# Activation, queries and keys transposed by Vector in 32x32 blocks and through DRAM, in a two-layer encoder

## The chip, the cores and the metric

The kernel runs on one core of a Trainium2 chip. The metric is the device time of one execution in microseconds, as the median of three runs; lower is better.

## The reference

Two layers act on x of 256 tokens by 2048. Each has a token mixer of four head groups and a SwiGLU channel mixer, both between RMS norms and with a residual:

```python
for l in range(DEPTH):
    h = rmsnorm(x, norm_mix_pre[l])
    proj = h @ w_in[l]
    a_q, a_k, a_v, b_glu, c_q, c_k, c_v, d_q, d_k, d_v = jnp.split(proj, split_at, axis=-1)
    out_a = diff_attention(a_q, a_k, a_v, diff_lambda[l], diff_subln[l], l)
    out_b = conformer_conv(b_glu, conv_dw[l], conv_dw_b[l], conv_ln_g[l], conv_ln_b[l],
                           conv_pw[l], conv_pw_b[l])
    out_c = gqa_axial_attention(c_q, c_k, c_v, gqa_q_norm[l], gqa_k_norm[l])
    out_d = neighbourhood_attention(d_q, d_k, d_v, na_rpb[l])
    mixed = jnp.concatenate([out_a, out_b, out_c, out_d], axis=-1) @ w_out[l]
    x = x + rmsnorm(mixed, norm_mix_post[l])
    h = rmsnorm(x, norm_ffn_pre[l])
    f = (jax.nn.silu(h @ ffn_gate[l]) * (h @ ffn_up[l])) @ ffn_down[l]
    x = x + rmsnorm(f, norm_ffn_post[l])
```

Groups A (differential attention, two maps of 64 per head), C (4 query heads over 2 key heads, normed and with rotary positions) and D (a neighbourhood window with a learned bias) have 4 heads of 128 each; B is a gated depthwise convolution of 31 taps over 512 channels, followed by a 512x512 product (`conv_pw`). The hidden width of the channel mixer is 5632. Everything is float32.

## The kernel before

All large products are weights times activations, in single-pass fp32r. Each weight is split into a high and a low part, each activation too, and three of the four products are summed in PSUM. The weights stream from DRAM: a `Raw` load (L201) brings two blocks of 128 rows by 1024 columns (1 MB; SP's queue, L214); `split_hi` (L222) makes the high part on Scalar (the names `whi`), `split_lo` (L231) the low part on Vector (`wlo`). A **unit** is one block of 128 x 1024, a **step** (L67) one unit times one tile of 128 tokens: six products of 128 x 512 (`products`, L297).

A layer runs four phases: the input projection in five column pairs in the order B, C, A, D, V, each 16 units by 2 token tiles (160 steps, written out at L1051); the output projection (two pairs, blocks in the order C, B, A, D in the first, L1062); gate and up (11 pairs of 512 columns of each, L1069); down (two pairs over 44 blocks, L1075). `run` (L345) walks through the steps. At each it calls the functions attached to the step (`pre`), advances the generators of the side work by one stretch (`tick`, L318), issues splits up to 7 units ahead (`NSPLIT`, `splits_to`, L242), which in turn issue the loads, and then the step's products. Where a step's activation isn't made yet, the planner's own clock is moved on (`wait`, L334). No engine reorders what it is given: the order in which Python emits is the order of each engine's queue, SP's included.

The generators do the side work: `norm_c`, `rope_a`, `evac_d` and `evac_v` (L827, L726, L921, L966) take a projected pair out of PSUM into the tiles `rotC`, `rotA`, `rotD`, `vAD`; `attn_c`, `attn_a`, `attn_d` (L863, L784, L934) transpose queries and keys and start a generator per head (`head_c`, `head_a`, `head_d`), which does scores (banks `sc`), softmax, and the transposes of the probabilities (`probs_transposed`, L771). A `yield` hands over until the next tick. Two PSUM banks each serve scores (`sc`) and transposes and small products (`tp`), two generators holding them in turn (`claim`, L148).

Queries and keys are needed with the head dimension on the partitions, and come out of the projection with the tokens there. `heads_transposed` (L752) has TensorE transpose four blocks of 128x128 into a `tp` bank, which Scalar copies into the tile `qkC`, `qkA` or `qkD`:

```python
for h in range(n):
    nc.tensor.transpose(b[:, h], src(tok)[:, h * P:(h + 1) * P], self.ident)
yield
nc.scalar.activation(dst[:, 0:n, tok * P:(tok + 1) * P], b[:, 0:n], AF.Copy)
```

In the channel mixer, `ffn_half` (L531) makes h of one 512-column block and one token tile. Vector then transposes it by 16 operations of 32x128 each (`quadrants`, L548), four between two yields; `split_hi_lo` (L194) turns the result `ht` into the two parts of `hT[j]`, which the down projection reads.

The convolution's weights (`pw`) and the position bias of group D (`load_bias`, L599, 16 small transfers, attached to step 108; `mask_bias`, L614, on Vector at step 120) go through SP's queue among the weights. SBUF has 14 large **slots** of 8 KB a partition (`slot`, L135), handed out in turn; the pool of temporaries has 4 buffers of 2 KB (`tmp`, L138), and the discarded output of a sum of squares (`junk`, L417) two of its own.

Of the kernel before, what the change touches and what calls it, by code (L numbers as in the profile page):

```python
# [11 lines left out]
F32 = mybir.dt.float32  # L12
# [7 lines left out]
P = 128  # L20
L = 2
S = 256
# [80 lines left out]
class Trunk:  # L103
    def __init__(self, ctx, tc, a):
# [10 lines left out]
        self.tp = pool("temps", 4)  # L115
# [301 lines left out]
    def square_sum(self, src, out, n=(512,), bias=0.0):  # L417
        junk = self.tp.tile([P] + list(n), mybir.dt.bfloat16, tag="junk", bufs=2, name=self.name("junk"))
        self.nc.scalar.activation(junk, src, AF.Square, bias=bias, accum_out=out)
# [111 lines left out]
    def ffn_half(self, phase, j, tok):  # L531
# [14 lines left out]
        self.mark("h", phase[1], j, tok)  # L546

    def quadrants(self, dst, src, q):  # L548

        qs = slice(32 * q, 32 * q + 32)  # L550
        for r in range(4):
            rs = slice(32 * r, 32 * r + 32)
            self.nc.vector.transpose(dst[qs, :, rs], src[rs, :, qs])
# [198 lines left out]
    def heads_transposed(self, dst, src, n):  # L752

        nc = self.nc
        for tok in range(T):
            yield from self.claim("tp")
            b = self.bank("tp", (4, P))
            for h in range(n):
                nc.tensor.transpose(b[:, h], src(tok)[:, h * P:(h + 1) * P], self.ident)
            yield  # L760
            nc.scalar.activation(dst[:, 0:n, tok * P:(tok + 1) * P], b[:, 0:n], AF.Copy)
            yield
            self.free("tp")
# [20 lines left out]
    def attn_a(self):  # L784
        qk = self.slot([2, 4, S], F32, "qkA")
        for i in range(2):
            yield from self.heads_transposed(qk[:, i], lambda t: self.rotA[:, t, i], 4)
        self.ptA = self.slot([4, T, S], F32, "ptA")
        work = self.slot([2, 2, T, S], F32, "workA")
        for h in range(4):  # L790
            yield from self.until(h - 1, "done_a", self.l)
            self.spawn(self.head_a(h, qk, work[:, h % 2]))
            yield

    def head_a(self, h, qk, p):
# [3 lines left out]
        for t in range(T):  # L799
            for m in range(2):  # L800
                rows = slice(m * 64, (m + 1) * 64)
                nc.tensor.matmul(banks[m][:, t], qk[rows, 0, h, t * P:(t + 1) * P], qk[rows, 1, h],
# [60 lines left out]
    def attn_c(self):  # L863
        qk = self.slot([6, S], F32, "qkC")
# [292 lines left out]
```

## Time and profile before

| | |
|---|---|
| median of 3 runs | 2179.55 us (2179.14 to 2179.74) |
| the profiled execution | 2179.21 us, of which the span of its trace is 2177.4 us |
| instructions in the trace | 25660 |
| HBM read, written | 414.40 MB, 8.39 MB (194 GB/s over the span) |
| POOL busy | 28.7 us, 38 instructions |
| DMA queue of the transfers, share of 16 engines | 56.5% |

The span runs from the first to the last recorded instruction; the execution's own time has some 1.8 us around it. Line numbers of instructions are nearly all L89, the helper through which every engine operation is issued, so groups are told apart by the names of their tiles: `acc<-whi,xT` is a product into an accumulator, `tp<-ident,rotD` a transpose of group D's queries or keys into a bank.

### The profile page before, as it was taken

To read this page: it belongs to the slowest core of one execution; us is meant where nothing else is said; L and a number is where in the kernel's file an instruction comes from. 1 tells how busy PE (TensorE), PEld (TensorE's weight loads), DVE (VectorE), ACT (ScalarE), POOL (GpSimd) and SP (SyncE) were. 2 spreads that over 40 slices of the span, in tenths; PEclk is the share of its full clock that TensorE was granted. 3 is DMA by queue.
4 is the path that set the end of the run, shared out by engine and by line. 5 is a ranking of instruction groups with operands and counts; after the bars stand their busy time and mean duration, and the time that the engine had idled before them with its cause. 6 is when DMAs were issued, how large, how long until landed. Compare 5 with 4: busy or idle time off the path is not lost.

```text
span 2177.4 us, 25660 instructions
## 1 busy us (share of the span) xinstructions
PE 2156.2 (99%) x9720; PEld 1780.7 (82%) x9720; DVE 1459.9 (67%) x2202; ACT 1083.2 (50%) x1420; POOL 28.7 (1%) x38
## 2 busy tenths in 40 slices
PE   8999999999999999999999999999999999999998
PEld 6888887888888888888878888878888888888886
DVE  5898555777777777444468975556677777764444
ACT  5556754544444444343465576554444444443432
POOL 0000000000000000000000000000000000000000
PEclk9999999999999999999999999999999999999999
DMA  7556446655555555555575553556555655555553
GB/s 281 197 173 181 171 148 222 210 196 193 193 194 194 193 194 194 213 193 194 211 238 186 188 186 135 208 189 222 193 191 180 209 193 193 179 208 213 193 216 132
DMA packets 170013, 424.46 MB, mean 195 GB/s; under 512 B 18593, under 2 KB 19105, under 8 KB 167585
## 3 DMA queue, kind: packets, MB, share of 16 engines
q1 hardware_dynamic: 169744, 422.79, 56.5%
q8 instruction: 76, 1.25, 0.2%
q14 instruction: 49, 0.39, 0.1%
q10 hardware_dynamic: 144, 0.03, 0.0%
HBM read 414.40 MB, written 8.39 MB: 194 GB/s over the span
## 4 chain that ended last, share of the span: by engine, by line
PE 96%; ACT 2%; DVE 1%; DMA 1%; issue 1%; SPq 0%; DVEq 0%; POOLq 0%; ACTq 0%
PE acc L89 92%; PE tp L89 3%; PE sc L89 1%; DMA raw<-in_w_in_dram 1%; ACT whi L89 1%; ACT workA L89 0%; ACT L89 0%; DVE xT L89 0%; DVE mx L89 0%; DVE wlo L89 0%; DVE x L89 0%; ACT xT L89 0%; ACT conv L89 0%; ACT qkD L89 0%; ACT junk L89 0%
## 5 line engine op out<-in xcount | busy, mean ns | idle before, releaser
L89 PE MATMUL acc<-whi,xT 128*128 128x512 f32 x4096 | 1292.9, 393 | 7.4 <-DVE xT L89 2.9
L89 PEld LDWEIGHTS acc<-whi,xT 128*128 128x128 f32 x4096 | 769.3, 188 | 172.3 <-DVE xT L89 5.5
L89 PE MATMUL acc<-wlo,xT 128*128 128x512 f32 x2048 | 798.7, 390 | 0.5 <-DVE wlo L89 0.5
L89 DVE SCALAR_TENSOR_TENSOR wlo<-raw,gains,whi 128x1024 fp32r<-128x1024 f32 x512 | 641.4, 1280 | 146.9 <-ACT whi L89 141.2
L89 ACT ACTIVATE whi<-raw,gains 128x1024 fp32r<-128x1024 f32 x512 | 574.7, 1147 | 269.6 <-PE acc L89 243.1
L89 DVE TENSOR_TENSOR wlo<-raw,whi 128x1024 fp32r<-128x1024 f32 x240 | 293.3, 1224 | 256.9 <-ACT whi L89 240.1
L89 PEld LDWEIGHTS acc<-wlo,xT 128*128 128x128 f32 x2048 | 385.1, 188 | 78.4 <-DVE wlo L89 1.0
L89 PE MATMUL acc<-whi,hT 128*128 128x512 f32 x1408 | 434.1, 389 | 0.0
L89 ACT ACTIVATE whi<-raw 128x1024 fp32r<-128x1024 f32 x240 | 253.6, 1060 | 296.1 <-PE acc L89 295.2
L89 PEld LDWEIGHTS acc<-whi,hT 128*128 128x128 f32 x1408 | 264.3, 188 | 54.9
L89 PE MATMUL acc<-wlo,hT 128*128 128x512 f32 x704 | 273.9, 389 | 0.0
L89 DVE STREAM_TRANSPOSE ht<-h 32x128 f32<-32x128 f32 x704 | 213.1, 303 | 10.9
L89 PEld LDWEIGHTS acc<-wlo,hT 128*128 128x128 f32 x704 | 132.1, 188 | 27.3
L89 ACT ACTIVATE hT<-ht 128x512 fp32r<-128x512 f32 x44 | 27.8, 632 | 244.3 <-DVE ht L89 244.3
L89 DVE SCALAR_TENSOR_TENSOR h<-acc,rstd,h 128x512 f32<-128x512 f32 x44 | 32.9, 747 | 110.8 <-ACT h L89 110.7
L89 DVE SCALAR_TENSOR_TENSOR conv<-uT,lc,conv 128x256 f32<-128x256 f32 x240 | 99.2, 477 | 0.0
L89 ACT ACTIVATE h<-acc,rstd 128x512 f32<-128x512 f32 x44 | 30.3, 688 | 81.6 <-PE acc L89 81.3
L89 DVE TENSOR_TENSOR hT<-ht,hT 128x512 fp32r<-128x512 f32 x44 | 30.4, 692 | 26.6 <-ACT hT L89 26.5
L89 ACT ACTIVATE junk<-acc 128x512 bf16<-128x512 f32 x32 | 19.1, 596 | 55.4 <-PE acc L89 53.3
L89 DVE TENSOR_TENSOR mg<-acc,gpost 128x512 f32<-128x512 f32 x32 | 21.4, 686 | 36.0 <-PE acc L89 19.3
L89 PE MATMUL acc<-whi,mixC 128*128 128x512 f32 x128 | 44.7, 402 | 0.0
L89 DVE TENSOR_TENSOR xT<-tp,xT 128x512 fp32r<-128x512 f32 x32 | 22.0, 687 | 30.2 <-ACT xT L89 30.2
(136 smaller groups left out, 992.0 us busy)
## 6 DMA issues: line engine op xcount, KB each, us to landing
raw<-in_ffn_gate_dram SPq DMA_DIRECT2D x176, 512.0 KB, 3.9
raw<-in_ffn_up_dram SPq DMA_DIRECT2D x176, 512.0 KB, 4.8
raw<-in_ffn_down_dram SPq DMA_DIRECT2D x88, 1024.0 KB, 4.9
raw<-in_w_in_dram SPq DMA_DIRECT2D x63, 1024.0 KB, 5.1
raw<-in_w_out_dram SPq DMA_DIRECT2D x32, 1024.0 KB, 5.0
raw<-in_w_in_dram SPq DMA_DIRECT2D x34, 512.0 KB, 4.8
x_spill<-x SPq DMA_DIRECT2D x6, 1024.0 KB, 7.7
x<-x_spill SPq DMA_DIRECT2D x6, 1024.0 KB, 8.4
```

The lines of the kernel that those rows point to most:

```text
L89: return f(*args, **kw)
```

## The change

**h.** `quadrants` goes. One Vector transpose of 128x512 turns every 32x32 block of h in place and sorts the blocks by row group (tile `blocks`); the tile is written to a DRAM buffer `hd[j]`. When both token tiles are there, four yields later, `turned` reads the buffer back with four transfers of 32 partitions each, rows of 512 bytes, into a tile `ht` of 128x1024; six yields later it is split into `hT[j]` by one operation of 1024 on Scalar and one on Vector, where there were two of 512 each.

**Queries and keys.** `heads_transposed` goes. `crossed` has Vector transpose the 32x32 blocks of each token tile into the slot `qk`, writes each token tile to DRAM (`hd`, L775) and, three yields later, reads both back in four transfers (L781) into the same slot; three yields later Scalar copies the queries into their place (`ptA` and `ptD`, whose slots are now taken before the crossing, or `rotC`). The keys are not copied: the score products read them from `qk`, where 32 consecutive keys of one head stand together and the next 32 follow after those of the other heads.

**Around it.** Temporaries 4 to 3, `junk` 2 to 1, the bias load from step 108 to 132, its mask from 120 to 142.

```diff
-        self.tp = pool("temps", 4)
+        self.tp = pool("temps", 3)
...
         yield
+        b = self.tmp([4, P], "blocks")
+        nc.vector.transpose(b.rearrange("p q (k n) -> p k q n", k=4),
+                            h.rearrange("p (k q n) -> p k q n", k=4, q=4))
+        yield
         if tok == 0:
-            self.hT[j] = self.slot([2, 4, S], F32R, "hT")
-        t = self.tmp([4, P], "ht")
+            self.hd[j] = self.pd.tile([S, 512], F32, name=self.name("h_blocks"))
+        nc.sync.dma_start(self.hd[j][tok * P:(tok + 1) * P, :], b.rearrange("p q m -> p (q m)"))
+        if tok == T - 1:
+            for _ in range(4):
+                yield
+            yield from self.turned(phase[1], j)
+
+    def turned(self, l, j):
+
+        t = self.tp.tile([P, 8, P], F32, tag="ht", bufs=1, name=self.name("ht"))
         for q in range(4):
-            self.quadrants(t, h.rearrange("p (k n) -> p k n", k=4), q)
-            yield
-        self.split_hi_lo([self.hT[j][:, i, :, tok * P:(tok + 1) * P] for i in range(2)], t)
...
+            src = self.hd[j][:, q * P:(q + 1) * P].rearrange("(t p) m -> p t m", p=32)
+            self.nc.sync.dma_start(t[32 * q:32 * q + 32], src)
+        for _ in range(6):
+            yield
...
-    def heads_transposed(self, dst, src, n):
...
+    def crossed(self, srcs, n, name, dst):
+
+        w = n * P
+        hd = self.pd.tile([S, w], F32, name=self.name(name))
+        qk = self.slot([2048], F32, name)
         for tok in range(T):
...
+            bt = qk[:, tok * 1024:tok * 1024 + w]
+            for h0 in range(0, n, 4):
+                m = min(4, n - h0)
+                out = bt.rearrange("p (q k n) -> p k q n", q=4, k=n)[:, h0:h0 + m]
+                src = srcs(tok, h0, m).rearrange("p (k q n) -> p k q n", k=m, q=4)
+                self.nc.vector.transpose(out, src)
+            yield
+            self.nc.sync.dma_start(hd[tok * P:(tok + 1) * P, :], bt)
+        for _ in range(3):
+            yield
+        qk = qk[:, 0:8 * n * 32].rearrange("p (t k n) -> p t k n", t=8, k=n)
+        for q in range(4):
+            src = hd[:, q * n * 32:(q + 1) * n * 32].rearrange("(t p) m -> p t m", p=32)
+            self.nc.sync.dma_start(qk[32 * q:32 * q + 32].rearrange("p t k n -> p t (k n)"), src)
+        for _ in range(3):
+            yield
+        for h, (out, m) in enumerate(dst):
+            q = qk[:, :, h * m:(h + 1) * m].rearrange("p t h n -> p h t n")
+            self.nc.scalar.activation(out.rearrange("p h (t n) -> p h t n", t=8), q, AF.Copy)
+        yield
+        return qk
...
     def attn_d(self):
-        qk = self.slot([2, 4, S], F32, "qkD")
-        for i in range(2):
-            yield from self.heads_transposed(qk[:, i], lambda t: self.rotD[:, t, i], 4)
         self.ptD = self.slot([4, T, S], F32, "ptD")
+        q = self.ptD[:, :, 0]
+        qk = yield from self.crossed(lambda t, h, n: self.rotD[:, t, h // 4], 8, "qkD", [(q, 4)])
...
-            nc.tensor.matmul(b[:, t], qk[:, 0, h, t * P:(t + 1) * P], qk[:, 1, h], start=True, stop=True)
+            nc.tensor.matmul(b[:, t], q[:, t * P:(t + 1) * P], k, start=True, stop=True)
...
-            self.steps[n0 + 108].pre += [lambda l=l: self.load_bias(l)]
-            self.steps[n0 + 120].pre += [self.mask_bias]
+            self.steps[n0 + 132].pre += [lambda l=l: self.load_bias(l)]
+            self.steps[n0 + 142].pre += [self.mask_bias]
```

Three places show how the order of the instructions moves. In the rows the numbers behind a name belong to the one tile of that name; the line at the start is that of the program. The first is SP's queue in the first layer, late in the input projection, from a load of pair D's weights on; the loads of 128x2x512 in pairs are those of pair V. Before:

```order
L214 DMA raw_1395<-in_w_in_dram 128x2x1024
L612 DMA bias_1430<-in_na_rpb_rev_dram 64x4x64 x16
L214 DMA raw_1484<-in_w_in_dram 128x2x512 x2
L214 DMA raw_1518<-in_w_in_dram 128x2x512 x2
L214 DMA raw_1613<-in_w_in_dram 128x2x512 x2
L214 DMA raw_1650<-in_w_in_dram 128x2x512 x2
L656 DMA pw_1733<-in_conv_pw_dram 128x4x512
L214 DMA raw_1752<-in_w_in_dram 128x2x512 x2
L214 DMA raw_1799<-in_w_in_dram 128x2x512 x2
```

and now:

```order
L214 DMA raw_1715<-in_w_in_dram 128x2x512 x2
L622 DMA bias_1766<-in_na_rpb_rev_dram 64x4x64 x16
L666 DMA pw_1803<-in_conv_pw_dram 128x4x512
L775 DMA qkD_1756<-qkD_1757 128x1024
L214 DMA raw_1832<-in_w_in_dram 128x2x512 x2
L775 DMA qkD_1756<-qkD_1757 128x1024
L214 DMA raw_1867<-in_w_in_dram 128x2x512 x2
L781 DMA qkD_1757<-qkD_1756 32x8x256 x4
L214 DMA raw_1960<-in_w_out_dram 128x2x1024
```

The bias transfers stood five loads ahead of `pw`; they stand right ahead of it now, and behind it come the two writes of group D's blocks (L775) and the four reads (L781), with one load between each.

The second is Scalar's queue of the same layer, at the copies of group D's queries and keys; `workA` are the exponentials of a head of group A, `conv` and `junk` the norm of the convolution. Before, the first of four copies out of a `tp` bank:

```order
L89 ACTIVATE ptA_1624<-tp_1858 128x512
L89 ACTIVATE whi_1879<-raw_1752,gains 128x1024
L89 ACTIVATE junk_1893,ss_1847<-conv_582,mu_1846 128x512
L89 ACTIVATE whi_1895<-raw_1752,gains 128x1024
L89 ACTIVATE whi_1916<-raw_1799,gains 128x1024
L89 ACTIVATE ptA_1624<-tp_1905 128x512
L89 ACTIVATE qkD_1845<-tp_1911 128x4x128
L89 ACTIVATE workA_1625,sm_1964<-sc_1940,mx_1963 128x256 x2
L89 ACTIVATE workA_1625,sm_1964<-sc_1941,mx_1963 128x256 x2
```

and now the one copy of the queries, which reads the slot that the four reads fill:

```order
L89 ACTIVATE ptA_1422<-tp_1910 128x512
L89 ACTIVATE ptD_1755<-qkD_1757 128x4x256
L89 ACTIVATE conv_582,mu_1934<-tp_1918 128x4x128
L89 ACTIVATE whi_1938<-raw_1715,gains 128x1024
L89 ACTIVATE whi_1956<-raw_1832,gains 128x1024
L89 ACTIVATE junk_1970,ss_1935<-conv_582,mu_1934 128x512
L89 ACTIVATE workA_1613,sm_1973<-sc_1950,mx_1972 128x256 x2
L89 ACTIVATE workA_1613,sm_1973<-sc_1951,mx_1972 128x256 x2
```

The copy now stands ahead of the second norm of the convolution, two weight splits and the exponentials, and takes 1024 elements a partition.

The third is the second layer's counterpart in the change, Scalar's queue first:

```order
L89 ACTIVATE ptA_9268<-tp_9740 128x512
L89 ACTIVATE ptD_9587<-qkD_9589 128x4x256
L89 ACTIVATE conv_8439,mu_9760<-tp_9745 128x4x128
L89 ACTIVATE whi_9764<-raw_9533,gains 128x1024
L89 ACTIVATE whi_9780<-raw_9660,gains 128x1024
L89 ACTIVATE ptA_9268<-tp_9775 128x512
```

and TensorE's queue at the transposes that it feeds and is fed by; the bank of the last row, `tp_9797`, is the one that `tp_9745` held:

```order
L89 MATMUL tp_9775<-ident,workA_9457 128x128 x4
L89 MATMUL acc_9621<-whi_9529,xT_8009 128x512
L89 MATMUL acc_9621<-wlo_9633,xT_8009 128x512
L89 MATMUL acc_9622<-whi_9529,xT_8009 128x512
L89 MATMUL acc_9622<-wlo_9633,xT_8009 128x512
L89 MATMUL acc_9621<-whi_9529,xT_8009 128x512
L89 MATMUL acc_9622<-whi_9529,xT_8009 128x512
L89 MATMUL tp_9797<-ident,conv_8439 128x128 x4
```

There the copy of D's queries stands between the last copies of group A's probabilities; before, the copies of D's queries and keys in this place each followed transposes of their own on TensorE.

## Rows read from the trace of the kernel before

**Rows 1.** Part 1 of the page: busy time, share and instructions by engine.

```profile
PE 2156.2 (99%) x9720; PEld 1780.7 (82%) x9720; DVE 1459.9 (67%) x2202; ACT 1083.2 (50%) x1420; POOL 28.7 (1%) x38
```

**Rows 2.** TensorE's waits; columns: total us, times, longest us.

```profile
PE tp L89 <- DVE workA L89: 0.2, 1, 0.2
```

**Rows 3.** The chain that ended last: start us, us, work.

```profile
191.63 1.06 PE sc L89 x8
...
384.19 701.14 PE acc L89 x3093
...
1253.08 0.86 PE tp L89 x4
```

**Rows 4.** Timeline of TensorE, from 238.41: start us, us, instruction.

```profile
238.41 0.60 PE L89 MATMUL tp<-ident,rotD 128*128 128x128 f32 x4
238.77 0.48 PE L89 MATMUL acc<-whi,xT 128*128 128x512 f32 x1
239.08 0.40 PE L89 MATMUL acc<-wlo,xT 128*128 128x512 f32 x1
```

**Rows 5.** Groups of TensorE's instructions by shape: busy us, mean ns.

```profile
L89 PE MATMUL tp<-ident,rotD 128*128 128x128 f32 x32 | 4.8, 274 | 0.0
...
L89 PE MATMUL tp<-ident,rotA 128*128 128x128 f32 x32 | 4.8, 272 | 0.0
L89 PE MATMUL tp<-ident,rotC 128*128 128x128 f32 x24 | 3.9, 272 | 0.0
```

**Rows 6.** Groups of Vector's instructions by shape.

```profile
L89 DVE STREAM_TRANSPOSE ht<-h 32x128 f32<-32x128 f32 x704 | 213.1, 303 | 10.9
...
L89 DVE TENSOR_TENSOR rotA<-rotA,rope 128x512 f32<-128x512 f32 x8 | 5.5, 692 | 0.3
```

**Rows 7.** Groups of Scalar's instructions by shape.

```profile
L89 ACT ACTIVATE whi<-raw,gains 128x1024 fp32r<-128x1024 f32 x512 | 574.7, 1147 | 269.6 <-PE acc L89 243.1 <-DMA raw<-in_w_in_dram 12.6 <-DMA raw<-in_ffn_up_dram 12.3
L89 ACT ACTIVATE whi<-raw 128x1024 fp32r<-128x1024 f32 x240 | 253.6, 1060 | 296.1 <-PE acc L89 295.2 <-DMA raw<-in_ffn_down_dram 0.8
...
L89 ACT ACTIVATE junk<-conv,mu 128x512 bf16<-128x512 f32 x4 | 2.9, 726 | 0.0
...
L89 ACT ACTIVATE conv<-tp 128x512 f32<-128x512 f32 x4 | 2.4, 609 | 0.0
```

**Rows 8.** Timeline of Scalar: four exponentials of a head of group A.

```profile
195.89 0.47 ACT L89 ACTIVATE workA<-sc,mx 128x256 f32<-128x256 f32 x1 [2.00 <-DVE mx L89]
...
197.61 0.21 ACT L89 ACTIVATION_READ_ACCUMULATOR workA<-sc,mx 128x1 f32 x1
```

**Rows 9.** Timeline of SP's queue around the bias loads of both layers.

```profile
164.28 11.89 SPq L612 DMA_DIRECT2D bias<-in_na_rpb_rev_dram  x16
...
1245.05 11.04 SPq L612 DMA_DIRECT2D bias<-in_na_rpb_rev_dram  x16
1256.19 2.92 SPq L214 DMA_DIRECT2D raw<-in_w_in_dram  x4
```

**Rows 10.** Timeline of TensorE beside them, both layers.

```profile
169.29 0.60 PE L89 MATMUL tp<-ident,rotA 128*128 128x128 f32 x4
...
1246.07 0.60 PE L89 MATMUL tp<-ident,workC 128*128 128x128 f32 x4
```

**Rows 11.** DMA issues, whole span: KB each, median us to landing.

```profile
bias<-in_na_rpb_rev_dram SPq DMA_DIRECT2D x32, 64.0 KB, 4.2
...
out_dram<-x SPq DMA_DIRECT2D x8, 256.0 KB, 2.4
```

**Rows 12.** DMA issues from 176.2 to 180, right behind the bias.

```profile
raw<-in_w_in_dram SPq DMA_DIRECT2D x4, 512.0 KB, 8.3
```

**Rows 13.** SP's waits; columns: total us, times, longest us.

```profile
SPq L214 <- DVE wlo L89: 1712.8, 346, 15.1
```

**Rows 14.** Stretches: busy time by engine, granted clock, DMA share, GB/s.

```profile
180.00:184.00 4.00, 4.00 (x22) 3.28 (x21) 3.96 (x9) 1.94 (x6) 0.00 (x0) 1.00 0.95 356
```

**Rows 15.** The same view of the last 8 us.

```profile
2170.00:2178.00 8.00, 0.00 (x0) 0.00 (x0) 3.48 (x6) 0.00 (x0) 0.55 (x1) 0.68 0.36 132
```

More of the change, by code (lines that the diff above doesn't have):

```diff
@@ L417, in square_sum @@
     def square_sum(self, src, out, n=(512,), bias=0.0):
-        junk = self.tp.tile([P] + list(n), mybir.dt.bfloat16, tag="junk", bufs=2, name=self.name("junk"))
+        junk = self.tp.tile([P] + list(n), mybir.dt.bfloat16, tag="junk", bufs=1, name=self.name("junk"))
         self.nc.scalar.activation(junk, src, AF.Square, bias=bias, accum_out=out)
@@ L784, in attn_a @@
     def attn_a(self):
-        qk = self.slot([2, 4, S], F32, "qkA")
-        for i in range(2):
-            yield from self.heads_transposed(qk[:, i], lambda t: self.rotA[:, t, i], 4)
         self.ptA = self.slot([4, T, S], F32, "ptA")
+        q = self.ptA[:, :, 0]
+        qk = yield from self.crossed(lambda t, h, n: self.rotA[:, t, h // 4], 8, "qkA", [(q, 4)])
         work = self.slot([2, 2, T, S], F32, "workA")
@@ L791, in attn_a, with head_a @@
             yield from self.until(h - 1, "done_a", self.l)
-            self.spawn(self.head_a(h, qk, work[:, h % 2]))
+            self.spawn(self.head_a(h, q[:, h], qk[:, :, 4 + h], work[:, h % 2]))
             yield
-    def head_a(self, h, qk, p):
+    def head_a(self, h, q, k, p):
         nc = self.nc
@@ L801, in head_a @@
                 rows = slice(m * 64, (m + 1) * 64)
-                nc.tensor.matmul(banks[m][:, t], qk[rows, 0, h, t * P:(t + 1) * P], qk[rows, 1, h],
+                nc.tensor.matmul(banks[m][:, t], q[rows, t * P:(t + 1) * P], k[rows],
                                  start=True, stop=True)
@@ L863, in attn_c @@
     def attn_c(self):
-        qk = self.slot([6, S], F32, "qkC")
-        yield from self.heads_transposed(qk[:, 0:4], lambda t: self.rotC[:, t, 0:512], 4)
-        yield from self.heads_transposed(qk[:, 4:6], lambda t: self.rotC[:, t, 512:768], 2)
+        q = [self.rotC[:, t, 0:512].rearrange("p (h s) -> p h s", h=2) for t in range(T)]
+        qk = yield from self.crossed(lambda t, h, n: self.rotC[:, t, h * P:(h + n) * P], 6, "qkC", [(x, 2) for x in q])
         self.mixT[2] = self.slot([2, 4, S], F32R, "mixC")
@@ L870, in attn_c @@
             yield from self.until(h - 1, "mix_c", self.l)
-            self.spawn(self.head_c(h, qk, work[:, h % 2]))
+            self.spawn(self.head_c(h, q[h // 2][:, h % 2], qk[:, :, 4 + h // 2], work[:, h % 2]))
             yield
@@ L896, in values, with head_c @@
         self.free("tp")
-    def head_c(self, h, qk, work):
+    def head_c(self, h, q, k, work):
         nc = self.nc
@@ L949, in head_d @@
         for t in range(T):
-            nc.tensor.matmul(b[:, t], qk[:, 0, h, t * P:(t + 1) * P], qk[:, 1, h], start=True, stop=True)
+            nc.tensor.matmul(b[:, t], q[:, t * P:(t + 1) * P], k, start=True, stop=True)
         yield
```

26 lines of the change are left out of this document (8 added, 18 removed).

## The prediction

> **What bounds the kernel now.** I read the busy times first: TensorE is at work for 99% of the span, Vector for 67%, Scalar for 50% [rows 1]. Then the list of TensorE's waits, to see whether that share hides any: the only wait in the attention stages is one of 0.2 us [rows 2]. Then the chain that ended last: it is TensorE's own products for nearly all its length, and one piece of it prices a product, 701.14 us for 3093, so 0.227 us [rows 3]. A change of this kernel therefore pays in only two ways: by what it takes off TensorE's queue, and by the waits that it puts there.
>
> I count in steps. A step is one block of 128 weight rows times one token tile, six products, so 1.36 us. A layer's input projection is 160 steps (pairs B, C, A, D, V), and T below is the moment at which TensorE reaches step 132 of a layer.
>
> **TensorE loses 88 transposes.** The three groups of rows are 32, 32 and 24 [rows 5]. Their price is the gap they make: four of them start at 238.41, the next product at 238.77, and the one behind that 0.31 later in place of 0.227, so 0.36 + 0.08 = 0.44 us for four [rows 4]. 88 / 4 x 0.44 = **9.7 us less**, all on the path. The transposes of h were on Vector already; the products, scores and other transposes stay as they are.
>
> **Vector and Scalar.** Vector drops 704 quarter transposes, 213.1 us, and gets 44 of 128x512 for h and some 20 a layer for queries and keys [rows 6]. A transpose of that shape isn't in the trace: between 0.30 (the quarter one) and twice the 0.69 us of an ordinary 128x512 operation [rows 6]; I take 0.69, nearest in shape, so 30 us for h, 15 for the rest. Scalar drops five 512-wide copies' worth of evacuations a layer and gets copies of 1024 elements. All of it is off the path: TensorE waits for neither engine. Were that cover gone (Vector late by a split), the price would be one product group.
>
> **Transfers in the channel mixer.** 22 times: two writes, four reads, in SP's queue among the weight loads. The loads wait there 1712.8 us in 346 waits, 5 us each, for a buffer that Vector frees [rows 13]; six issues of at most 0.73 us in the 43.5 us of one 512-column block fit into that. The result is first read in the down projection. I cost it at nothing; if a read were late, Scalar's split of h would hold the weight splits behind it, which are issued some seven steps ahead (9.5 us).
>
> **The D group's transfers are where I expect the loss.** The SP rows in the section on the change show it: the 16 bias transfers now stand at step 132, right ahead of the convolution's weights (pw), D's two writes with a weight load between, another load, and D's four reads. SP works in order. Step by step:
>
> - The bias block takes 11.89 us in one layer and 11.04 in the other [rows 9]. It began 2.3 us before TensorE reached its step in the first layer (step 110 is at 169.29, less 12 products, 166.57, against 164.28) and 1.4 us before in the second (1246.07 + 0.44 against 1245.05) [rows 9, 10]. I keep these leads, as the same kind of load stands ahead of it: it ends at T + 9.6 in both.
> - Then pw, write 1 and a load of two parts precede write 2. Four such issues took 2.92 us right behind the bias [rows 9], so write 2 goes out at T + 12.5.
> - Transfers issued right behind the bias landed after 8.3 us [rows 12]; 3 MB lie in the queue up to write 2, at 356 GB/s 8.4 us [rows 14]. Write 2 is down at T + 20.8, and only then may the reads go: the last of four 2.2 us later, and 4.2 us to land as a bias transfer does, the nearest in shape (short runs, part of the partitions) [rows 11]. **Read back at T + 27.2.**
> - Scalar's copy of D's queries is issued at step 141 and waits for all four. Behind it in Scalar's queue stand weight splits, convolution and the exponentials of group A (rows in the section on the change).
>
> What TensorE needs of that: in layer 0 the next A head's scores (step 147) need the score banks, which Scalar frees only after the copy (1.06, as long as a 1024-wide split), conv with its accumulator read (0.8), two splits (2.3), a square (0.9) and eight exponential instructions (195.89 to 197.82, 1.9): 7.0 us [rows 7, 8]. From step 132 to there TensorE has 90 products (20.4), two value products (0.86 each), five groups of transposes (0.44 each) and a score group (1.06) [rows 3, 4]: T + 25.4. Wait: 27.2 + 7.0 - 25.4 = **8.8 us**. In layer 1 the transpose ahead of step 143 needs a bank that Scalar's conv row right behind the copy frees: 1.9 us; TensorE arrives after 66 products, two value products and three groups of transposes at T + 18.0. Wait: 27.2 + 1.9 - 18.0 = **11.1 us**. Nothing later gives this back, since TensorE has no other idle time there.
>
> Bounds of this pair: with writes and reads landing as the quickest row, 2.4 us [rows 11], read back is at T + 19.5, the waits 1.1 and 3.4; with the queue drained first (4 MB from T + 9.6) and reads at 8.3, T + 33.5 and waits of 15.1 and 17.4. The sum takes 19.9, nearest to the rows taken behind a bias block; 4.5 and 32.5 go into the range.
>
> The Trainium skill, page DMA: Bandwidth & Descriptors, section on the anatomy of one DMA, gives a transfer about 2.0 us plus its bytes at 436 GB/s. By that, as an estimate, a 512 KB write takes 3.2 us and a read 2.6 us, read back is at T + 20.5, and the sum would end 13 us lower; the 8.3 us behind the bias speaks against it here.
>
> **C, A and the output projection.** C's and A's reads stand behind a weight load each; I find Scalar held some 2 to 3 us, and TensorE's first scores of C three steps (4.1 us) behind the copies. In the second layer the last output transposes of A follow their products by 18 products instead of 30. From nothing to 2 us a layer; I take 1.
>
> A wait of 9 or 11 us may also cost clock: the granted clock, 1.00 throughout the work, averages 0.68 in the last 8 us, where TensorE had nothing to do [rows 15]; no row shows products after such a fall, and I take zero. The page TensorE: Matmul & The Clock Gate of the Trainium skill, Part 1, says that an idle TensorE falls to half its clock and has to work to regain it; by that each long wait costs more than itself, and the sum would lie higher.
>
> **Sum.** The profiled execution took 2179.2 (2177.4 span, 1.8 around it), 0.3 under the median of the runs. 2179.2 - 9.7 + 19.9 + 2 = 2191.4, against the median 2191.7; forecast **2191.5**.
>
> **Rivals.** What a measurement can tell from no change is some 0.2%, 4.4 us, so 2175.2 to 2183.9 counts as the same.
>
> 1. *The read back is in time; faster.* It decides at T + 18.4 in layer 0 and T + 16.1 in layer 1. SP isn't tied to steps: if the loads ahead of the bias are free 9 to 11 us earlier than in the old place, nothing waits. For it: the slots that the bias takes were released some ten steps before. Against: in both layers the bias began only 1.4 and 2.3 us ahead. Time: 2179.5 - 9.7 + 0 to 2 = 2170 to 2172. Chance 0.20.
> 2. *Short transfers; little or no change.* The waits are 4.5 to 10 us in all, since the writes move in another direction than loads or the queue is emptier than behind the old bias block. 2174.5 to 2182. Chance 0.23; a third of it falls under 2175.2.
> 3. *Strided keys; slower.* The keys are now read in runs of 32 elements. No product before does so. If that halved the rate, the score products would cost twice their time, 80 of them at some 0.27 to 0.43 us: 25 us more, 2195 without and 2215 with D's waits. The score group's 1.06 us for eight records [rows 3] would double. Chance 0.05.
> 4. *More than intended:* Vector's 180 us freed could speed up the channel mixer. TensorE waits for nothing there, so it can't; no chance of its own.
>
> The forecast itself has 0.52, its own range 2182 to 2204. Faster: 0.20 + 0.07; same: 0.16 and a little of the forecast's low end, 0.18; slower: 0.55. The range for 8 in 10 runs from rival 1 to the forecast's upper part, 2168.5 (rival 1, and a microsecond for the price of a transpose) to 2203.
>
> **What would show it.** Right: transposes of rotA, rotC and rotD are gone from TensorE; the list of its waits gets two entries near step 143 and step 147 of the layers, of 6 to 14 us, ended by Scalar, while Scalar's longest wait is for a transfer into qkD; SP shows bias, pw and D's transfers back to back. Wrong: Scalar waits for qkD under 3 us (rival 1 or 2), score groups longer than 1.1 us (rival 3), or long waits elsewhere, at C's or A's first scores above all, which I put at 1 us a layer, or in the channel mixer, which I put at nothing.

## The result, and the profile after

The changed kernel takes 2234.16 us as the median of 4 runs (2228.52 to 2237.36), against 2179.35 for the kernel before beside it: 1.0249 of its time, interval 1.0236 to 1.0262. It is slower, as forecast, but by 54.8 us where 12 were forecast, and 31 us above the range. The profiled execution is the fastest of the four, 2228.52, with a span of 2226.7; what follows is read from it, and its span is 49.3 us over that of before.

Busy times, part 1 of the page [rows 1]:

```profile
span 2226.7 us, 25117 instructions
...
PE 2163.2 (97%) x9632; PEld 1783.7 (80%) x9632; DVE 1283.0 (58%) x1544; ACT 1083.4 (49%) x1380; POOL 28.7 (1%) x38
```

Vector has lost 177 us of work and TensorE 88 transposes, and the span has grown. TensorE's busy time grew too, with less to do. Its waits say where, [rows 2] having been the only such row before (PE is TensorE, ACT Scalar, DVE Vector, SPq SP's queue; the numbers are total us, times, longest us):

```profile
PE tp L89 <- ACT conv L89: 14.2, 1, 14.2
PE sc L89 <- ACT workA L89: 11.4, 2, 11.2
PE tp L89 <- DVE mixC L89: 9.5, 2, 5.0
PE sc L89 <- ACT rotC L89: 5.3, 2, 3.2
...
PE sc L89 <- ACT workC L89: 1.9, 2, 1.7
```

Placed in the program by the order of TensorE's queue, these are, in the first layer, 2.2 us at C's first scores (step 103), 1.9 at A's (126), 5.0 at step 136 (for Vector, mixC) and 11.2 at step 147; in the second, 3.2 (step 104), 4.6 (140, for Vector) and 14.2 (143). Behind all but the wait of 1.9 us the granted clock falls to 0.50 for a while. Stretches of the first layer: length, busy time of PE, PEld (TensorE's weight loads), DVE, ACT and POOL, granted clock, DMA share, GB/s:

```profile
246.00:257.00 11.00, 0.00 (x0) 0.00 (x0) 3.75 (x6) 5.46 (x12) 0.00 (x0) 0.70 0.40 80
257.00:264.00 7.00, 6.86 (x17) 4.81 (x18) 4.47 (x11) 6.96 (x15) 0.59 (x1) 0.50 0.59 218
264.00:271.00 7.00, 7.00 (x36) 5.79 (x35) 2.66 (x3) 6.96 (x16) 0.00 (x0) 0.99 0.18 49
```

TensorE did nothing from 246 on; the granted clock averages 0.70 there, and in the 7 us behind, 17 records are worked off at 0.50, so 1.2 GHz, in place of 36 at 0.99. Summed in stretches of 1 us over the two attention stages (140 to 300 and 1255 to 1400), TensorE is idle for 42.8 us, and busy time x (1 - granted clock) comes to 14.0 us: 56.8, where before it was 0.2. Less 9.7 for the transposes that makes 46.9 of the 49.3; the other 2.4 I can't place, unless the transposes were worth less than 9.7.

Ahead of nearly all of it Scalar stands at its copies of the queries; the waits at steps 136 and 140 are Vector's, below:

```profile
ACT ptD L89 <- DMA qkD<-qkD: 32.5, 2, 16.8
ACT rotC L89 <- DMA qkC<-qkC: 20.1, 2, 11.3
...
ACT ptA L89 <- DMA qkA<-qkA: 16.3, 2, 8.4
```

And this is SP's queue for D in the first layer (start, us, transfers; L622 bias, L775 D's writes, L781 its reads), and the copy that waits for it:

```profile
217.06 10.60 SPq L622 DMA_DIRECT2D bias<-in_na_rpb_rev_dram  x16
227.77 0.53 SPq L666 DMA_DIRECT2D pw<-in_conv_pw_dram  x1
228.35 0.50 SPq L775 DMA_DIRECT2D qkD<-qkD  x1
228.96 2.03 SPq L214 DMA_DIRECT2D raw<-in_w_in_dram  x2
231.04 0.96 SPq L775 DMA_DIRECT2D qkD<-qkD  x1
...
242.62 1.81 SPq L781 DMA_DIRECT2D qkD<-qkD  x4
```

```profile
250.52 1.06 ACT L89 ACTIVATE ptD<-qkD 128x1024 f32<-128x1024 f32 x1 [15.70 <-DMA qkD<-qkD]
```

The bias, pw, write, load, write and reads stand as the order said. The times to landing of D's transfers, writes and reads:

```profile
qkD<-qkD SPq DMA_DIRECT2D x4, 512.0 KB, 9.8
qkD<-qkD SPq DMA_DIRECT2D x8, 256.0 KB, 5.8
```

But the bias begins late, and so does Vector's transposing of D, both waiting for TensorE's last products with C's values (13.5 us of SP's waits are for that, in two; Vector's are in its group):

```profile
SPq L622 <- PE tp L89: 13.5, 2, 9.5
```

```profile
L89 DVE STREAM_TRANSPOSE blocks<-h 128x512 f32<-128x512 f32 x44 | 31.0, 705 | 0.0
...
L89 DVE STREAM_TRANSPOSE qkD<-rotD 128x512 f32<-128x512 f32 x8 | 5.2, 689 | 8.4 <-PE tp L89 8.4
```

The addresses in the built program say why: the bias gets the slot in which C's probabilities lie (`workC`) in both layers, and D's tile `qkD` that of `rotC`, whose values the last C heads read. In the kernel before, the bias of the first layer had the slot of an `x` tile, free since x was transposed early in the projection.

### The profile page after: what moved, and what is told of

It is laid out like the page before. It is cut to its first block, busy times and chain, and to the rows that moved or that the text cites. A ratio compares the mean times of both kernels' runs of the same rounds, so it can differ in the third digit from the quotient of the medians.

```text
span 2226.7 us, 25117 instructions
## 1 busy us (share of the span) xinstructions
PE 2163.2 (97%) x9632; PEld 1783.7 (80%) x9632; DVE 1283.0 (58%) x1544; ACT 1083.4 (49%) x1380; POOL 28.7 (1%) x38
## 4 chain that ended last, share of the span: by engine, by line
PE 88%; DVE 5%; DMA 3%; ACT 2%; issue 1%; SPq 0%; ACTq 0%; DVEq 0%; POOLq 0%
PE acc L89 84%; PE tp L89 2%; DVE wlo L89 2%; DMA qkD<-qkD 2%; PE sc L89 1%; DVE conv L89 1%; DMA qkC<-qkC 1%; ACT whi L89 1%; DMA qkA<-qkA 1%; DVE rotC L89 0%; SPq L781 0%; ACT workA L89 0%; DVE xT L89 0%; DVE rope L89 0%; ACT junk L89 0%
## 5 line engine op out<-in xcount | busy, mean ns | idle before, releaser
L89 DVE TENSOR_TENSOR hT<-ht,hT 128x1024 fp32r<-128x1024 f32 x22 | 27.0, 1226 | 153.8 <-ACT hT L89 153.8
L89 ACT ACTIVATE hT<-ht 128x1024 fp32r<-128x1024 f32 x22 | 23.3, 1060 | 119.1 <-DMA ht<-h_blocks 119.0
L89 PE MATMUL acc<-whi,mixB 128*128 128x512 f32 x128 | 41.9, 396 | 0.0
L89 PE MATMUL acc<-whi,mixD 128*128 128x512 f32 x128 | 41.6, 391 | 0.0
```

The source lines that it names most:

```text
L89: return f(*args, **kw)
```

## The experiments

Times are medians; the change's 2234 is the mark. Runs called "alone" leave the other groups on TensorE, so they compute the same.

### Which part

`e1` is the kernel before with h's new path only, `e2` the change with h's old path (its edit; that of `e1` is the same lines the other way, with the change's buffers):

```diff
-        self.tp = pool("temps", 3)
+        self.tp = pool("temps", 4)
...
-        b = self.tmp([4, P], "blocks")
-        nc.vector.transpose(b.rearrange("p q (k n) -> p k q n", k=4),
...
+        t = self.tmp([4, P], "ht")
+        for q in range(4):
+            self.quadrants(t, h.rearrange("p (k n) -> p k n", k=4), q)
+            yield
```

> The kernel before with the new path of h alone (Vector transposes of 128x512, two writes and four reads through DRAM); queries and keys are transposed by TensorE as before, and the bias stands at step 108. Theory (the loss lies in the attention stages, and h costs nothing because TensorE waits for neither Vector nor the transfers in the channel mixer): 2179 to 2180 us, no new wait of TensorE. Rival (the reads hold Scalar and with it the weight splits, or the extra traffic slows the loads): 2184 us or more, with waits of TensorE for whi in the channel mixer.

> The changed kernel with the old path of h (16 quarter transposes on Vector), temporaries and junk buffers as before; queries and keys cross DRAM. Theory: all of the loss is here, 2226 to 2238 us, with the same seven or eight waits of TensorE near steps 103, 136 and 147 (first layer) and 104, 140 and 143 (second). Rival (the two parts hurt each other): clearly under 2220 us.

2179.62 us for h alone (ratio 0.9991 to 1.0014) and 2230.66 for queries and keys alone, with the waits of the change (14.1, 12.3, 9.5 us). All of the loss is in the attention stages, and h costs and brings nothing. Single groups, made from the change by putting `heads_transposed` back for the others, C and D in `e9`, C and A in `e10`; here D's lines:

```diff
     def attn_d(self):
+        qk = self.slot([2, 4, S], F32, "qkD")
+        for i in range(2):
+            yield from self.heads_transposed(qk[:, i], lambda t: self.rotD[:, t, i], 4)
         self.ptD = self.slot([4, T, S], F32, "ptD")
-        q = self.ptD[:, :, 0]
-        qk = yield from self.crossed(lambda t, h, n: self.rotD[:, t, h // 4], 8, "qkD", [(q, 4)])
```

> The changed kernel (h through DRAM, pools, bias at step 132) with only group A crossing; queries and keys of C and D are transposed by TensorE again. Theory (A costs little by itself, since the waits stand at C's first scores, at D's slot and at D's copy): 3.5 us less for 32 transposes, at most 2 us of wait back, 2176 to 2180 us. Rival (Scalar's copy of A's queries, held 8 us for the reads, makes TensorE wait once the others are gone): waits of 3 us or more in each layer with stretches at half clock, 2184 us or more.

> The changed kernel with only group D crossing; C and A are transposed by TensorE again, the bias stays at step 132. Theory (D's read back carries most of the loss): waits for Scalar and Vector of 20 to 36 us in all near steps 136 to 147, 6 to 10 us of half clock, less 3.5 us of transposes: 2200 to 2222 us. Rival (the three crossings make each other late, and D alone is in time): D's waits under 10 us in all, under 2192 us.

A alone: 2181.69, a wait of 3.8 us in one layer and none in the other, between the two theories. D alone: 2200.64, with waits of 7.5 and 12.6 us. The whole loses 54.8, A and D alone 2.5 and 21.5; no run has C alone, so the 30.8 that are left belong to C and to what the groups do to each other. In the order, C's first scores move from step 97 to 103 and its last value products from steps 126 and 129 to 133 and 134; those are what the bias and D's tile wait for. In the run with D alone no such wait is left on Vector.

### The bias, the slots and the queue

`e3` moves the bias behind D's reads:

```diff
-            self.steps[n0 + 132].pre += [lambda l=l: self.load_bias(l)]
-            self.steps[n0 + 142].pre += [self.mask_bias]
+            self.steps[n0 + 140].pre += [lambda l=l: self.load_bias(l)]
+            self.steps[n0 + 148].pre += [self.mask_bias]
```

> The changed kernel with the bias loads attached to step 140 and the mask to 148, so that SP issues the 16 bias transfers behind group D's four reads; the slots of D's queries and keys stay those that C's last value products still read. Theory of the prediction (the bias block in front of D's writes makes D's wait): D's waits of 11.2 and 14.2 us fall to under 5 us together, with their stretches at half clock, and the time to 2195 to 2207 us; the waits of 5.0 and 4.6 us at steps 136 and 140 stay, since Vector still waits for the slot there. Rival (the bias only fills time that the queue loses anyway, and D's transfers take as long without it): D's waits stay over 8 us each, 2220 us or more.

2220.07 (2216.1 to 2224.0), 13 us above the range of the theory. D's waits fell from 25.4 to 12.0 us, in the theory's direction, but not to 5: pw had got the slot that the bias had left, and stood in SP's queue in its place (16.3 us in two waits for TensorE). The 9.6 us for Vector stayed.

`e4` gives the pool a fifteenth slot, paid for with the split lookahead; `e5` is its control, `e6` has the bias early besides:

```diff
-SLOTS = 14
+SLOTS = 15
-NSPLIT = 7
+NSPLIT = 6
```

> The changed kernel with 15 slots in place of 14, paid for by a split lookahead of 6 units in place of 7. The bias then gets a slot that is free long before, and D's queries and keys one whose last reader is a score product of C, not a value product. The order in SP's queue stays (bias, pw, D's writes and reads). Theory of the slots (bias and Vector's transposes of D wait for the slots of C's probabilities and values, which makes the waits of 5.0 and 4.6 us and delays the bias by 4 and 9 us): the waits at steps 136 and 140 fall under 1 us, D's to 5 to 9 us each, 2198 to 2212 us. Rival (the order of the transfers alone): the waits at 136 and 140 go, if at all, by 2 us, and D's stay at 10 us or more, 2220 us or more.

> Control for the run with 15 slots: the kernel before, with 15 slots and a split lookahead of 6 units. Theory (six units of lookahead, some 8 us, cover what Scalar and Vector do between): 2179 to 2181 us. Rival (the 9 us of waits for wlo in the run with 15 slots come from the shorter lookahead alone): 2184 us or more.

> The changed kernel with 15 slots, lookahead 6, and the bias loads back at step 108 (mask 142); D's queries and keys again get the slot of C's values, so Vector waits there. Theory (D's end is set by the read back, and the bias block of 11 us in front of D's writes is what makes it late; Vector's wait for the slot only takes its share of the same time): D's waits of 16 and 18 us fall under 6 us each, the time to 2205 to 2220 us. Rival (Vector's slot sets it): D's waits stay over 10 us, 2228 us or more.

The control missed: 2205.07, so the shorter lookahead alone costs the kernel before 25.6 us, and the totals of `e4` (2234.09) and `e6` (2223.87) can't be set against 2234. Their waits can:

```profile
PE tp L89 <- ACT conv L89: 18.4, 1, 18.4
PE acc L89 <- ACT whi L89: 15.8, 2, 14.1
PE acc L89 <- DVE wlo L89: 9.1, 5, 2.4
...
PE tp L89 <- DVE mixC L89: 2.6, 1, 2.6
```

Vector's wait for its slot was gone, the wait for mixC fell from 9.5 to 2.6, and D's two grew to 18.4 and 14.1 from 14.2 and 11.2: what TensorE doesn't wait for at step 136 it waits for at step 147. The end of D's transfers is what counts. The bias began at 214.77, which is T + 4.9, so no earlier against TensorE than in the change (T + 4.7; T is TensorE's step 132), since its new slot too was held, by the convolution. With the bias at step 108 (`e6`), D's waits fell to 0.8 and 7.5, and the time, set against `e4` with its equal slots and lookahead, by 10.2 us, although Vector waited for its slot again (10.2 us).

`e8` issues the crossings' transfers from GpSimd's queue:

```diff
-        self.sync, self.queue = nc.sync, nc.scalar
+        self.sync, self.queue, self.pq = nc.sync, nc.scalar, nc.gpsimd
...
-            self.nc.sync.dma_start(hd[tok * P:(tok + 1) * P, :], bt)
+            self.nc.pq.dma_start(hd[tok * P:(tok + 1) * P, :], bt)
...
-            self.nc.sync.dma_start(qk[32 * q:32 * q + 32].rearrange("p t k n -> p t (k n)"), src)
+            self.nc.pq.dma_start(qk[32 * q:32 * q + 32].rearrange("p t k n -> p t (k n)"), src)
```

> The changed kernel with the 36 transfers of queries and keys issued from GpSimd's queue, not SP's; the transfers of h stay on SP. Theory (the read back is late because it stands in SP's order behind the bias and behind loads that wait for buffers): D's writes go out as soon as Vector has made the blocks, read back is 10 us earlier, D's waits under 3 us each, C's under 1 us; the waits of 5.0 and 4.6 us for Vector stay: 2190 to 2205 us. Rival (the transfers are slow by themselves, or from this queue): D's waits stay over 8 us, 2220 us or more.

2213.30: between the two. The writes went out 0.3 us behind Vector and landed after 4.8, but the reads, issued at 225.64, took 12.7 to land, next to the loads on SP's queue. D's waits were 8.7 and 7.2. Order alone isn't what makes these transfers late.

```profile
qkD<-qkD POOLq DMA_DIRECT2D x4, 512.0 KB, 4.8
...
qkD<-qkD POOLq DMA_DIRECT2D x8, 256.0 KB, 12.7
```

### The clock

Products with a tile of zeros, added into the open accumulator ahead of each wait (`s` is the step, `n` their number); the sums don't change:

```diff
...
+    def zeros(self, s, n):
+        b = self.acc[s.phase, s.pair, s.tok, 0]
+        for _ in range(n):
+            self.tc.nc.tensor.matmul(b[:, 0:64], self.ident, self.zero, start=False, stop=False)
...
```

> The changed kernel with products of zeros added into the open accumulator at the six places where TensorE waits 2 us or more (steps 103, 136, 147; 104, 140, 143), some 9 tenths of each wait, at an estimated 0.1 us each from the transposes' 0.11. They change no sum and no wait of another engine, and keep TensorE at work. Theory (14 us of the loss are products at half clock behind the waits): the granted clock stays at 1.00 over most of these stretches, and the time falls by 8 to 14 us, to 2215 to 2226 us. Rival (the clock is no cost of its own, since what follows a wait waits again anyway): 2228 to 2240 us.

> As the run with products of zeros, with half as many at each place, since one took 0.22 us there and they ran past the waits: now they fill some 9 tenths of each wait. Theory (the products behind a wait run at half clock, 14 us of the loss): the granted clock stays at 1.00 behind the filled waits, waits and zeros together take what the waits took, and the time is 8 to 14 us below the changed kernel's, 2218 to 2228 us. Rival (nothing is gained, because the next link is late by just as much): 2230 us or more.

The first, 2253.66, overran: a zero product leaves two records and took twice my estimate, 76.6 us in all. With half as many, 2231.17, no better than the change itself (2228 to 2237). The helper's line is L91 here; each zero product has two records:

```profile
L320 PE MATMUL acc<-zero,ident 128*128 128x64 f32 x334 | 37.9, 274 | 0.0
```

```profile
PE sc L91 <- ACT workC L91: 4.3, 2, 3.2
PE sc L91 <- ACT workA L91: 3.9, 3, 3.5
PE tp L91 <- ACT conv L91: 3.6, 1, 3.6
```

The clock stayed at 1.00 behind the waits of steps 103, 136, 104 and 140; at step 147 the zeros took 10.6 us and a wait of 3.5 was left, 14.1 where 11.2 were, at 143 13.1 and 3.6 for 14.2. At A's first scores of the first layer the wait grew too, from 1.9 to 3.2 us, and behind it the clock now fell. So what the clock gave back was waited for at a later place. Most of the 14 us at half clock was no cost of its own: 9.1 of it lay ahead of another wait. The other 4.9 us lie behind D's waits, where nothing waits next; the zeros didn't fill those to the end, and what these 4.9 cost isn't settled by this run.

### Scalar's place at the copies

In `crossed`, the yields between the reads and the copy; 3 became 9 in all groups (`e12`), in D alone (`e13`), in C and A alone (`e14`):

```diff
             self.nc.sync.dma_start(qk[32 * q:32 * q + 32].rearrange("p t k n -> p t (k n)"), src)
-        for _ in range(3):
+        for _ in range(9):
             yield
```

> The changed kernel with nine yields in place of three between the reads and Scalar's copy of the queries, in all three groups, so that the copy stands some six steps (8 us) later in Scalar's queue and less of other work stands behind a copy that isn't ready. Theory (TensorE waits because Scalar, in order, stands at the copy with splits, convolution and exponentials of others behind it): Scalar's waits for C's and A's reads fall from 18 us a layer to under 4, D's from 16 to 8 each, TensorE's waits at the first scores of C and A vanish, D's fall under 6 us each; the waits for Vector near steps 136 and 140 stay: 2192 to 2208 us. Rival (the later heads are missed by the output projection instead): new waits behind step 160, 2220 us or more.

> The changed kernel with only group D's copy six yields later; C and A as in the changed kernel, and D's tile and the bias keep the slots that C's values and probabilities hold. Theory (Scalar standing at the copy makes D's waits, the slots those of 5.0 and 4.6 us): D's waits fall from 25 us to under 8 in all, the waits near steps 136 and 140 stay within 1 us, C's 5 us stay: 2200 to 2212 us. Rival (the slots are behind both): D's waits stay over 15 us in all, 2222 us or more.

> The changed kernel with the copies of C and A six yields later and D's copy where it is; by this D's tile and the bias get slots that nothing late still reads. Theory (two causes side by side): C's and A's waits and those near steps 136 and 140 are gone, D's copy still stands 8 to 14 us in Scalar's queue and D's waits stay at 8 to 25 us in all: 2190 to 2212 us. Rival (the slots alone, with C's lateness, did it): D's waits under 4 us in all, 2184 us or less.

`e12`: 2180.00, better than its theory, and level with before (0.9993 to 1.0016). The transfers are the same, though the bias and D's tile get other slots, for which Vector no longer waits; six steps later the transfers are nearly there, and Scalar's waits for them are these, in place of 68.9 us:

```profile
ACT ptD L89 <- DMA qkD<-qkD: 4.7, 2, 3.0
...
ACT rotC L89 <- DMA qkC<-qkC: 1.0, 1, 1.0
```

`e13`, in which bias and D's tile keep the held slots: 2215.18, 3 us above its theory's range.

```profile
PE tp L89 <- DVE mixC L89: 9.6, 2, 5.0
PE sc L89 <- ACT rotC L89: 5.0, 2, 2.8
...
PE acc L89 <- ACT rotD L89: 3.4, 1, 3.4
PE sc L89 <- ACT workC L89: 3.3, 1, 3.3
```

```profile
ACT ptD L89 <- DMA qkD<-qkD: 2.6, 2, 1.4
```

D's waits are gone (Scalar's at its copy fell from 32.5 to 2.6 us), those for Vector and at C's scores are nearly unchanged: the two causes are apart. `e14`, where the slots are free (Vector waits for none) and D's copy stands as it did: 2199.56.

```profile
PE tp L89 <- DVE mixC L89: 14.5, 1, 14.5
PE tp L89 <- ACT ptA L89: 7.5, 1, 7.5
```

```profile
ACT ptD L89 <- DMA qkD<-qkD: 24.3, 2, 16.2
```

Each of the two waits is now in one piece, 14.5 and 7.5, with Scalar at D's copy behind both. The name in the row (mixC) is that of whoever came last. In the longer one Vector's mixC itself waited for Scalar, whose copy of mixC began 2.0 us behind the start of D's copy (1323.57), with one split between:

```profile
1325.96 0.42 DVE L89 TENSOR_TENSOR mixC<-tp,mixC 128x256 fp32r<-128x256 f32 x1 [17.20 <-ACT mixC L89]
```

Set side by side: D's copy moved alone is worth 19 us, with C's and A's copies early (54.8 to 35.7) as with them late (20.1 to 0.8); C's and A's copies, with the slots that come free by moving them, are worth 35. No run frees the slots alone, so what they cost by themselves isn't shown.

### A version that gains

With 9, 6 and 9 yields for C, A and D, and with 9, 7 and 12; and the latter with the bias at step 140 (mask 148):

```diff
-        for _ in range(3):
+        for _ in range(9 if name == "qkC" else 7 if name == "qkA" else 12):
             yield
```

> All three copies later, by 9, 6 and 9 yields for C, A and D in place of 3, which gives the output projection of the second layer its heads in an order nearer to that of before. Theory: the transposes' 9.7 us show as far as no wait takes them: waits of 2 to 6 us in all, 2172 to 2178 us. Rival (the crossings shift the same few us of waits elsewhere): 2179 us or more.

> As the run with 9, 6 and 9, with 9, 7 and 12 yields: D's copy three steps later still. Theory: Scalar's wait for D's reads goes from some 2 us a layer to none, TensorE's waits are 2 to 6 us in all, 2172 to 2178 us. Rival (D's heads now come too late for the last part of the output projection): waits behind step 176, 2180 us or more.

> The run with the copies later by 9, 7 and 12 yields, with the bias at step 140 and its mask at 148, so that the 16 transfers stand behind D's reads. Theory (with the copies late, Scalar no longer stands, and the bias block costs nothing where it is): the same within 2 us, 2173 to 2177 us. Rival (the block still holds D's or C's transfers for TensorE): 2171 us or less; or the mask now comes too late for D's first scores, 2179 us or more.

2184.25 (11 runs, in its rival's range), **2174.99** (11 runs, 2174.40 to 2177.60, ratio 0.9982, interval 0.9973 to 0.9991) and 2187.84. The second beats both kernels, by 4.5 us against before. Its page, its transfers and copy for D, and the waits in the attention stages:

```profile
span 2172.9 us, 25118 instructions
```

```profile
205.91 10.59 SPq L622 DMA_DIRECT2D bias<-in_na_rpb_rev_dram  x16
...
218.61 0.99 SPq L775 DMA_DIRECT2D qkD<-qkD  x1
...
226.22 1.81 SPq L781 DMA_DIRECT2D qkD<-qkD  x4
```

```profile
243.43 1.04 ACT L89 ACTIVATE ptD<-qkD 128x1024 f32<-128x1024 f32 x1
```

```profile
PE sc L89 <- ACT workA L89: 1.4, 2, 1.2
PE sc L89 <- ACT vAD L89: 1.3, 1, 1.3
PE tp L89 <- DVE mixC L89: 1.1, 1, 1.1
```

The bias block still stands in front of the writes, and write 2 takes 7.6 us to the reads; the copy at 243.43 no longer waits. Idle time in the two stages is 3.8 us and half clock 1.7: 9.7 - 5.5 = 4.2, and the span is 4.5 below that of before. By the same sum the transposes are worth 9.8 us here, the prediction's price, but some 8 in `e12` and `e14`, 7 in the change, 6 in `e15` and 4 in `e13`: no run has them without other waits, and their size is shown as some 4 to 10 us only. Moving the bias behind D's reads made this version 12.9 us slower, as the last of the three ways in its expectation had it (the mask too late), and by the same mechanism on another engine: the mask on Vector now stands at a transfer that isn't there, with other groups' softmax behind it.

```profile
DVE bias L89 <- DMA bias<-in_na_rpb_rev_dram: 20.7, 2, 11.1
```

The 9 us between the first two versions come from a few steps in the place of the heads; TensorE's small waits in the first (2.7, 2.9, 1.7, 1.5 us and others) are spread over the stage, and I haven't traced them one by one.

### What h's path is worth

The control with 15 slots, with h's path changed:

> The control with 15 slots and a lookahead of 6 units, with h through DRAM as in the changed kernel (queries and keys by TensorE). Theory (with the quarter transposes Vector was too busy for six units, and the new path gives it back 180 us): the 25 waits for wlo of the control go, 2179 to 2183 us. Rival (six units are too few in any case): 2200 us or more.

2191.76 against the control's 2205.07, between the two theories. TensorE's waits for Vector's splits, control and this run:

```profile
PE acc L89 <- DVE wlo L89: 18.0, 25, 2.4
```

```profile
PE acc L89 <- DVE wlo L89: 8.6, 5, 2.4
```

The 180 us taken off Vector are worth 13 us where the lookahead is six units, and nothing where it is seven.

## Why the prediction was wrong, point by point

**Right:** for D, the places and the mechanism. The transposes were worth something near the 9.7 us (4 to 10 by the versions above); h's path is hidden; a Vector transpose of 128x512 takes 0.70 us (0.69 taken); the long waits stand at steps 147 and 143, ended by Scalar at its copy of D's queries; strided keys cost nothing (D's score products take 379 ns, before and after), so that rival is out.

```profile
L89 PE MATMUL sc<-qkD 128*128 128x256 f32 x32 | 8.2, 379 | 0.0
```

```profile
L89 PE MATMUL sc<-qkD,ptD 128*128 128x256 f32 x32 | 7.9, 379 | 0.0
```

**Wrong, first: when D's transfers begin.** The step "It began 2.3 us before TensorE reached its step ... I keep these leads" failed. I let the bias begin as early as in its old place, since the loads ahead of it were of the same kind, and took its slots to have been "released some ten steps before" (rival 1). In the old place SP waits for no slot at the bias. In the new one the bias got slots that C's heads still held: from TensorE's products, T is 212.35 in the first layer and 1314.8 in the second, and the bias began at T + 4.7 and T + 8.4, not T - 2.3 and T - 1.4. SP was free for it at T + 0.6 and T - 1.2; the 4.0 and 9.5 us from there are the wait for the slot. The rest of the term, step by step, first and second layer:

| | predicted | measured |
|---|---|---|
| bias begins | T - 2.3, T - 1.4 | T + 4.7, T + 8.4 |
| bias block | 11.9, 11.0 | 10.6, 10.5 |
| its end to write 2 | 2.9 | 3.4, 3.4 |
| write 2 to the reads | 8.3 | 11.6, 10.0 |
| reads to the copy | 6.4 | 7.9, 8.2 |
| read back | T + 27.2 | T + 38.2, T + 40.5 |
| copy to TensorE's go-on | 7.0, 1.9 | 6.6, 1.7 |

Fed with the measured read back and go-on, the prediction's own sum gives 19.4 and 24.2 us of delay from T on, 43.6 in place of 19.9; the trace shows 40.2 there (the waits at steps 136 and 147, 140 and 143, and the half clock between them). Most of the difference is TensorE's own way to these places, which took 26.0 and 20.6 us in place of 25.4 and 18.0 (in the second layer A's scores, 2.0 us, stand in it). The upper bound, T + 33.5, was passed too (the figures given for it add up to T + 32 only): it bounded the hops, not their start.

The start isn't all of it. In `e14` the bias began at T - 3.3 and T + 2.2, and D's copy still not before T + 35.1 and T + 34.3; in the first layer pw waited 4.8 us for a slot of its own, and write 2 took 11.8 to land. With D alone (`e10`) the copy came at T + 29.5 and T + 30.9, and D's two waits were 20.1 us, close to the 19.9 of the sum, though in part by luck, since read back was 2 to 4 us later than it says. Of the page DMA: Bandwidth & Descriptors of the Trainium skill, section on the anatomy of one DMA, the estimate was 3.2 us for such a write and 2.6 for a read. The section speaks of transfers issued by GpSimd; D's went out from SP, and landed after 9.8 (median of four) and 5.8. Issued from GpSimd (`e8`) they landed after 4.8 and 12.7, so beside this kernel's loads the trace doesn't agree either way.

**Wrong, second: C and A at 1 us a layer.** C's first scores lost 9.8 us in the two layers (waits of 2.2 and 3.2, and 4.5 of half clock behind them), A's 1.9. Scalar stood 20.1 us at C's copies. I had counted 2 to 3 us there, by the place in the queue, without pricing the two hops as I did for D; from the issue of the second write to the copy C's took 13 to 17 us, A's 17 to 19 and D's 18 to 20.

**Wrong, third: no clock.** I took zero, since "no row shows products after such a fall". The rows of after show products at a clock of 0.50 behind the longer waits, with 14.0 us lost in all. That is the size; as a cost most of it fell together with the next wait.

The page TensorE: Matmul & The Clock Gate of the Trainium skill, Part 1, which says that a TensorE left idle drops to half its clock, agrees with the trace: 0.50 behind the longer waits. The trace adds that what this costs depends on whether something else is waited for next.

In ledger form, spans, by where TensorE lost the time (which isn't what it would get back were one cause removed): -9.7 (transposes) + 40.2 (D up to its last wait) + 4.9 (half clock behind it) + 9.8 (C) + 1.9 (A) - 0.2 (idle before) = 46.9, of 49.3. Against the sum of the prediction (2191.4, with 2228.5 measured in the profiled execution) that is 20.3 too little for D, 4.9 for the clock, 9.7 for C and A, and the 2.4 that aren't placed, less the 0.2.

## What to carry to other kernels

Before costing a transfer by its place in a queue, find out which buffer its destination gets and who reads that buffer last: a step moved later may land in a slot that is freed later still. An instruction that consumes a round trip through DRAM belongs into an in-order engine's queue only where the round trip is over, here some 13 to 20 us behind the write; one that stands there early holds everything behind it, and moving it by four to nine steps changed 54.8 us of loss into a gain of 4.5, with the same transfers and with buffers that came free by the move. And a wait removed ahead of a longer one may be worth nothing, as in `e4` and with the zero products: follow the chain to the last.

## What the runs showed that I had not expected

- A TensorE at half clock ahead of another wait cost nothing measurable: 37.9 us of zero products kept the clock at 1.00 behind four of six waits, and the time stayed (2231 against 2228 to 2237).
- Reads issued from a queue of their own were not quicker: a median of 12.7 us to landing for D's reads of 256 KB from GpSimd's queue, beside SP's loads, against 5.8 on SP's queue, where no load went out behind them for 10 us. That the loads beside them are the reason isn't shown.
- One unit of split lookahead less costs the kernel before 25.6 us, with 25 waits of at most 2.4 us for Vector's splits; with Vector 180 us less busy, 12.6.
- The changed kernel's own runs spread by 8.8 us (2228.52 to 2237.36), those of the kernel before by 0.8. What moves them isn't shown.
